# Dilated attention + S5 decoder layer: near values from a time-ordered copy of x, first weights in one transfer, last stores by halves

## The chip, the cores and the metric

One core of one Trainium2 chip runs the whole layer as a single program. The metric is device time in microseconds, the median of several executions. Engines are named as the profile names them: PE is TensorE (matmul; PEld its weight loads), DVE is VectorE, ACT is ScalarE, POOL is GpSimd, SP is SyncE, which here only issues DMAs.

## What is computed

A decoder layer on 512 tokens of width 1024. `x @ w_in` gives q, k and v for three dilation groups of attention (8 heads of 64 each), the input `u` of a state space model (SSM), and two sets of gate logits. Cut to what matters here:

```python
proj = x @ w_in[layer]
q, k, v = ...                      # (b, s, 3 groups, 8 heads, 64)
u, gate_logits = ...               # (b, s, 512), (b, s, 2, 1024)
for g, (window, dilation) in enumerate(((128, 1), (512, 4), (2048, 16))):
    o_g, lse_g = dilated_group_attention(q[:, :, g], k[:, :, g], v[:, :, g], window, dilation)
attn = sum over g of softmax(lse)_g * o_g
y_ssm = GLU(GELU(s5_ssm(u, ...))) @ w_ssm_br
h = layer_norm(ALPHA * x + (gates * (attn @ w_attn_br, y_ssm)) @ w_out)
x = layer_norm(ALPHA * h + (silu(h @ w_ff_gate) * (h @ w_ff_up)) @ w_ff_down)
```

Group 0 (window 128, dilation 1, "near") attends over tokens in the order of time, 128 at a time. Groups 1 and 2 attend over tokens of the same phase modulo 4 or 16.

## The kernel before, in words

**Tokens.** The host stores x with its tokens ordered by phase (time modulo 4). That is the order that groups 1 and 2 want. The near group wants time order, and the kernel reorders its q, k and v on the chip.

**Products.** Every product is done in a split form: a matrix is cut into a high half (rounded to fp32r) and a low half (the rest), and three matmuls `hi*hi`, `hi*lo`, `lo*hi` accumulate in one PSUM bank (`mm3`, lines 186 to 188). The function `split` makes the halves: ACT casts the high half (line 179), DVE subtracts it from the source to get the low half (line 180). For x and the first weights (of `u`) they are made at the start; for all other weights a class `Weights` loads units of 128x2048 by SP's queue into one of two `raw` buffers and splits each unit in two views `whi`/`wlo` of 128x1024, in three rotating slots. View n belongs to step n.

**Steps.** The table STEPS lists the projection tiles in the order of the program: steps 0 to 3 are `u` (done together by `u_tiles`), steps 4 to 7 the near values, steps 8 to 19 gates, then near k and q, then the other groups. Each step is 24 matmuls of 128x512 (`proj_tile`, or `v_tiles`). Other work is hung on steps by `at_step(n, ...)` and run by `run_fill(n)` in the middle of step n, or by `run_fill(n + 0.5)` at its end. Each engine executes its own instructions strictly in the order in which the program emits them.

**Near values before** (`v_near`, `v_turn`). Step 4 + hp makes 128 channels of v by 512 tokens in phase order (weights are the stationary operand, x the moving one). ACT copies the bank into time order (`vt`), and one step later PE transposes the four 128x128 blocks of `vt` into a bank `tv` (line 745), which ACT copies into `v`. The values of groups 1 and 2 are made by `v_tiles` instead: x blocks of 128 tokens are stationary, 512 columns of weights move, four banks are filled over four steps, and the result stands with tokens on the partitions, so nothing is transposed.

**The SSM's preparation** runs on DVE between these splits, as a list `late` of about two hundred small instructions (tiles `t16s`, `pw`, `bb`, then `zs`, `zd`, `ca`, `a`), of which `late.take` emits some now and then and `drip` a quota each half step. `make_pm` transposes `zs` on PE (16 transposes, tiles `pt`, line 522) and ACT copies them to `pmT`; `state_inputs` (tiles `sb`) needs `pmT` at the ends of steps 7 and 8.

**The end.** After the last matmul the last 128 rows are normalised: `norm_first` and `norm_second` are DVE instructions of 128x512, and `store` sends the rows in two halves of 64 by two queues. Before, the last quarter of the columns is scaled by ACT and finished by POOL (line 1265) while DVE does the rest.

Of the kernel before, what the change touches and what calls it, by code (L numbers as in the profile page):

```python
# [57 lines left out]
def as_phases(z):  # L58

    return z.rearrange("p (c r) -> p r c", r=4)  # L60
# [91 lines left out]
def emit(ctx, tc, i, out):  # L152
# [21 lines left out]
    dense, scores, turned, outs = ring(0, 1, 2), ring(3, 4), ring(5, 6), ring(7)  # L174
    pairs_ = ring(6, 7, 4, 5)

    def split(hi, lo, src, scale=None):
        if scale is None:
            act.copy(hi, src)  # L179
            dve.tensor_tensor(lo, src, hi.bitcast(F32), op=ALU.subtract)  # L180
        else:
            act.mul(hi, src, scale)  # L182
            dve.scalar_tensor_tensor(lo, src, scale, hi.bitcast(F32), op0=ALU.mult, op1=ALU.subtract)
# [40 lines left out]
    for n in range(2, N_GLU, 2):  # L224
        kind, g, un, _ = STEPS[n]
        if kind == "u":
            w.add(i["w_in"][1], 8)
        elif kind == "g":
            w.add(i["w_in"][20 + un], 8)
        else:  # L230
            w.add(i["w_in"][2 + 6 * g + 2 * "kqv".index(kind) + un], 2 if kind == "v" and g else 8)
    for un in range(2):
        w.add(i["w_glu"][un], 4)
    for un in range(4):
# [21 lines left out]
        queue.dma_start(wu[k0 // 4][:, k0 % 4 : k0 % 4 + k1 - k0],  # L256
                        i["w_in"][k0 // 4].rearrange("p (k c) -> p k c", k=4)[:, k0 % 4 : k0 % 4 + k1 - k0])

    for e in cols256:
        act.dma_start(wu[0][:, 0, e], i["w_in"][0][:, e])  # L260
    dve.memset(warm[:, 0:P], 0.0)
    act.activation(wact, warm[:, 0:1], AF.Exp)
    wb_ = dense("warm_b")
# [22 lines left out]
    zt = prep[:, 1024:2048]  # L286
    dmat = sa.tile([P, 8, 16], F32, name="dmat")
    sp.dma_start(sm, i["ssm_bc"])
    w.load()
    sp.dma_start(dmat, i["dmat"])  # L290
    sp.dma_start(bgate, i["bgate"])
    sp.dma_start(ident, i["ident"])
    sp.dma_start(rope, i["rope"])
    sp.dma_start(masks.rearrange("p n k -> p (n k)"), i["masks"].rearrange("p n k -> p (n k)"))

# [171 lines left out]
    for k in range(KT):  # L467
        if k == 0:

            (xh, uh), (xl, ul) = ((z[0][:, 0, :] for z in (xp[n], wup[n])) for n in range(2))  # L470
            xs, us = xr[0][:, 0:512], wu[0][:, 0, :]
            c0, c1 = cols256
            dve.tensor_copy(uh[:, c0], us[:, c0])
            act.copy(xh[:, c0], xs[:, c0])
            dve.tensor_copy(xh[:, c1], xs[:, c1])
            act.copy(uh[:, c1], us[:, c1])
            tt(xl, xs, xh.bitcast(F32), ALU.subtract)
            tt(ul, us, uh.bitcast(F32), ALU.subtract)
            late.take(4)
            continue  # L480
        split_x(k)
        split(wup[0][k // 4][:, k % 4], wup[1][k // 4][:, k % 4], wu[k // 4][:, k % 4])
        late.take(4 if k < 2 else 10)
# [248 lines left out]
        else:  # L732
            tt(dv[:, hp, :], cq, sw, ALU.add)

    def v_near(dv, ws, hp, mid):

        b = proj_tile(ws, f"pv0{hp}", mid)
        vt = at.tile([P, 512], F32, tag="cq", name=f"vt{hp}")
        act.copy(as_phases(vt), by_phase(b))
        return dv, vt, hp  # L740

    def v_turn(dv, vt, hp):
        b = turned(f"tv0{hp}")
        for blk in range(4):
            pe.transpose(b[:, 128 * blk : 128 * blk + 128], vt[:, 128 * blk : 128 * blk + 128], ident)
        act.copy(dv[:, :, 128 * hp : 128 * hp + 128], b.rearrange("p (b c) -> p b c", b=4))

    def v_tiles(dv, ws, j, g, mid):

        if j == 0:  # L750
            ssm["vb"] = [bank(7, f"pv{g}{tb}") if tb == 2 else dense(f"pv{g}{tb}") for tb in range(4)]
        for tb, b in enumerate(ssm["vb"]):
            if tb == 2:
                mid()
            for kk in range(2):
                k = 2 * j + kk
                mm3(b, kslice(xp, k, slice(128 * tb, 128 * tb + 128)), (ws[0][:, kk, :], ws[1][:, kk, :]), k == 0, k == KT - 1)
            if j == 3:
                act.copy(dv[:, tb, :], b)

# [175 lines left out]
    drip(9, 20, 1600)  # L936
    drip(20, 28, 500)
    at_step(3.5, u_turn)
    at_step(6, make_pm)
    for r in range(2):  # L940
        for m in range(2):
            at_step(7.5 + r, state_inputs, r, m)
# [39 lines left out]
    for hp in range(NPAIR):  # L982
        at_step((58, 59, 60, 61)[hp], merge_pair, hp)

    for _ in range(3):
        w.split()
        late.take(12)
    u_tiles()
    run_fill(3.5)
    for n in range(4, N_GLU):  # L990
        kind, g, un, c = STEPS[n]

        def mid(n=n):
            run_fill(n)

        if kind == "g":
            gate_tile(w.views[n], un, c, mid)
        else:
            if un == 0 and c == 0:
                dv = home({"k": (1, "g3", "g0"), "q": (8, 2, 1), "v": (3, "g1", 0)}[kind][g], f"{kind}{g}")  # L1000
                if qkv[g] is None:
                    qkv[g] = [None] * 3
                qkv[g]["qkv".index(kind)] = dv.rearrange("p (b c) -> p b c", b=4)
            dv = qkv[g]["qkv".index(kind)]
            if kind == "v" and g == 0:
                at_step(n + 1, v_turn, *v_near(dv, w.views[n], 2 * un + c, mid))
            elif kind == "v":
                v_tiles(dv, w.views[n], 2 * un + c, g, mid)
            else:
                qk_tile(dv, w.views[n], g, 2 * un + c, f"{kind}{g}", mid)  # L1010
        w.release()
        run_fill(n + 0.5)
# [244 lines left out]
    mv = mvs[NTT - 1]  # L1257
    dve.bn_aggr(mv[:, 0:2], bsts[NTT - 1])
    rstd(mv)
    for cs in reversed(halves):  # L1260
        norm_first(end, mv, lnb2, cs)

    cs = quarters[3]
    act.mul(end[:, cs], end[:, cs], mv[:, 3:4])
    pool.tensor_tensor(end[:, cs], end[:, cs], lnb2[:, 1, cs], op=ALU.add)
    for q, c in (((sp, act), halves[0]), ((act, sp), quarters[2])):
        norm_second(end, mv, lnb2, c)
        store(q, NTT - 1, end, c)
    store((sp, act), NTT - 1, end, cs)


def constants():
# [21 lines left out]
def layout(a):  # L1294
    x = a["x"][0][TOKENS]
    w = a["w_in"][0]
    hd = np.concatenate([np.arange(0, 16), np.arange(32, 48), np.arange(16, 32), np.arange(48, 64)])
    perm = (np.arange(NH)[:, None] * 64 + hd[None, :]).reshape(-1)
    parts = [w[:, 4608:5120]]
    for g in range(3):  # L1300
        parts.append(w[:, 1536 + 512 * g : 1536 + 512 * g + 512][:, perm])
        parts.append(w[:, 512 * g : 512 * g + 512][:, perm])
        parts.append(w[:, 3072 + 512 * g : 3072 + 512 * g + 512])
    parts.append(w[:, 5120:])

    def units(m, nk, cols):
        k, c = m.shape
        t = m.reshape(k // (nk * P), nk, P, c // cols, cols).transpose(0, 3, 2, 1, 4)
        return np.ascontiguousarray(t.reshape(-1, P, nk * cols))

    def pairs(m, nk, cols):
        k, c = m.shape
        t = m.reshape(nk, P, c // (2 * cols), 2, cols).transpose(2, 1, 3, 0, 4)
        return t.reshape(-1, P, 2 * nk * cols)

    glu = np.stack([a["w_glu"][0][:, :512].reshape(512, 4, P), a["w_glu"][0][:, 512:].reshape(512, 4, P)], 2)
    gu = np.stack([a["w_ff_gate"][0].reshape(D, NFF, P), a["w_ff_up"][0].reshape(D, NFF, P)], 2).reshape(D, 2 * DFF)
    parts = [units(p, 4, 512) if j in (0, 6, 9) else pairs(p, 8, P) for j, p in enumerate(parts)]

    def state(m):  # L1320
        return m.reshape(2, 8, 2, 64, *m.shape[2:]).transpose(2, 3, 1, 0, *range(4, m.ndim + 2)).reshape(P, NGP, *m.shape[2:])

    are, aim = state(a["ssm_a_re"][0]), state(a["ssm_a_im"][0])
    ldt = state(np.broadcast_to(a["ssm_log_dt"][0][:, None], (NG, 64)))
    br, bi = (state(a[n][0]).reshape(P, 256) for n in ("ssm_b_re", "ssm_b_im"))
    cr, ci = (state(a[n][0].transpose(0, 2, 1)).reshape(P, 256) for n in ("ssm_c_re", "ssm_c_im"))
    dm = np.zeros((4, 32, 8, 16), np.float32)
    d = a["ssm_d"][0].reshape(8, 4, 16)
    for h in range(16):
        dm[:, h, :, h] = d[:, :, h].T  # L1330
    xT = x.T.reshape(KT, P, S).transpose(1, 0, 2).reshape(P, KT * S)
    return {
        "x": x, "xT": xT, "w_in": np.concatenate(parts), "w_br": np.concatenate([units(a[n][0], 4, 256).reshape(2, 2, P, 1024).transpose(0, 2, 1, 3).reshape(2, P, 2048)
                                for n in ("w_ssm_br", "w_attn_br")]),
        "w_glu": pairs(glu.reshape(512, 1024), 4, 256), "w_out": units(a["w_out"][0], 4, 512)[[0, 2, 1, 3]],
        "w_gu": pairs(gu, 8, P), "w_dn": units(a["w_ff_down"][0], 2, 1024),
        "bgate": a["b_gate"][0].reshape(16, P).T, "ssm_small": np.stack([are, aim, ldt], 1),
        "ssm_bc": np.stack([np.stack([br, bi], 1), np.stack([cr, ci], 1)], 1),
        "dmat": dm.reshape(P, 8, 16), "ln1": np.stack([a["ln1_g"][0], a["ln1_b"][0]]),
        "ln2": np.stack([a["ln2_g"][0], a["ln2_b"][0]]),  # L1340
    }
# [24 lines left out]
```

## Time and profile before

| | us |
|---|---|
| median of 3 executions | 861.52 (861.26 to 861.63) |
| the profiled execution's own time | 861.88 |
| its span, first to last instruction | 860.1 |
| PE busy in the span | 850.1 (99%) |
| DVE busy | 485.7 (56%) |
| ACT busy | 292.2 (34%) |
| POOL busy | 26.5 (3%) |

The span is what the trace shows; 1.78 us of the profiled execution lie around it. Positions in the trace are microseconds from the span's start. Shares of busy time are averages over the whole span and say little of one stage.

### The profile page before, as it was taken

How to read it: one execution, taken by the hardware profiler on the slowest of the kernel's cores; microseconds unless marked ns; L12 is line 12 of the kernel's file. 1: busy time of each engine (PE TensorE's matmuls, PEld its weight loads, DVE VectorE, ACT ScalarE, POOL GpSimd, SP SyncE). 2: the span in 40 equal slices, each digit the busy share in tenths (PEclk: the TensorE clock that was granted, in tenths of full speed). 3: DMA queues.
4: the chain of work that ended last, by engine and by line, in shares of the span. 5: the costliest groups of instructions: out<-in, count | busy, mean ns of one | idle time of the engine just before them, and what ended most of it. 6: DMA issues, size and time to landing. Idle time of an engine off the chain costs nothing.

```text
span 860.1 us, 11317 instructions
## 1 busy us (share of the span) xinstructions
PE 850.1 (99%) x4586; PEld 701.6 (82%) x4586; DVE 485.7 (56%) x948; ACT 292.2 (34%) x477; POOL 26.5 (3%) x28
## 2 busy tenths in 40 slices
PE   9999999999999999999999999999999999999996
PEld 7878888887778888888888898888888888888885
DVE  7965899974665546356795863444433444222237
ACT  5364331155443344553251342222222222211111
POOL 0000000000000000000000600000000000000005
PEclk9999999999999999999999999999999999999999
DMA  9723421325121312112624142222222222322204
GB/s 340 189 83 105 122 98 50 125 89 180 50 98 51 101 62 86 50 56 92 244 99 147 50 147 98 98 98 98 94 93 94 92 92 94 136 96 96 95 0 98
DMA packets 24628, 90.06 MB, mean 105 GB/s; under 512 B 6400, under 2 KB 11264, under 8 KB 15488
## 3 DMA queue, kind: packets, MB, share of 16 engines
q1 hardware_dynamic: 22704, 86.59, 29.4%
q10 hardware_dynamic: 1872, 2.74, 0.9%
q8 instruction: 36, 0.59, 0.3%
q14 instruction: 16, 0.13, 0.0%
HBM read 84.87 MB, written 4.46 MB: 104 GB/s over the span
## 4 chain that ended last, share of the span: by engine, by line
PE 93%; DVE 3%; DMA 2%; ACT 1%; issue 0%; SPq 0%; DVEq 0%; ACTq 0%
PE fg L188 9%; PE fg L186 9%; PE fg L187 9%; PE dn L187 4%; PE dn L188 4%; PE dn L186 4%; PE pg L186 3%; PE pg L187 3%; PE pg L188 3%; PE pk L188 3%; PE pq L187 3%; PE pq L188 3%; PE pk L187 3%; PE pk L186 3%; PE pq L186 3%; PE pv L186 2%
## 5 line engine op out<-in xcount | busy, mean ns | idle before, releaser
L180 DVE TENSOR_TENSOR wlo<-raw,whi 128x1024 fp32r<-128x1024 f32 x134 | 164.3, 1227 | 200.1 <-ACT whi L179 200.0
L179 ACT CAST whi<-raw 128x1024 fp32r<-128x1024 f32 x134 | 140.1, 1047 | 221.5 <-PE dn L188 73.3
L186 PE MATMUL fg<-hh,whi 128*128 128x512 f32 (+1 forms) x376 | 141.3, 376 | 0.0
L187 PE MATMUL fg<-hl,whi 128*128 128x512 f32 (+1 forms) x376 | 141.2, 375 | 0.0
L188 PE MATMUL fg<-hh,wlo 128*128 128x512 f32 (+1 forms) x376 | 141.2, 375 | 0.0
L187 PEld LDWEIGHTS fg<-hl,whi 128*128 128x128 f32 x376 | 70.8, 188 | 12.9
L188 PEld LDWEIGHTS fg<-hh,wlo 128*128 128x128 f32 x376 | 70.8, 188 | 12.8
L186 PEld LDWEIGHTS fg<-hh,whi 128*128 128x128 f32 x376 | 70.8, 188 | 12.7
L187 PE MATMUL dn<-wlo,ff 128*128 128x512 f32 x168 | 65.4, 389 | 0.0
L186 PE MATMUL dn<-whi,ff 128*128 128x512 f32 x168 | 65.4, 389 | 0.0
L188 PE MATMUL dn<-whi,ff 128*128 128x512 f32 x168 | 65.4, 389 | 0.0
L186 PE MATMUL pg<-x_hi,whi 128*128 128x512 f32 x128 | 50.7, 396 | 0.0
L187 PE MATMUL pg<-x_lo,whi 128*128 128x512 f32 x128 | 49.9, 390 | 0.0
L188 PE MATMUL pg<-x_hi,wlo 128*128 128x512 f32 x128 | 49.9, 390 | 0.0
L182 ACT ACTIVATE ff<-fth 128x512 fp32r<-128x512 f32 x22 | 14.0, 634 | 102.7 <-DVE fth L315 102.7
L315 DVE TENSOR_TENSOR fth<-fth,fg 128x512 f32<-128x512 f32 x22 | 15.1, 687 | 56.9 <-PE fg L188 56.8
L791 ACT ACTIVATE pt<-pt,st 128x256 f32<-128x256 f32 (+1 forms) x64 | 31.0, 485 | 43.5 <-DVE st L789 43.5
L186 PE MATMUL pk<-x_hi,whi 128*128 128x512 f32 x96 | 37.8, 394 | 0.0
L186 PE MATMUL pq<-x_hi,whi 128*128 128x512 f32 x96 | 37.8, 394 | 0.0
L188 PE MATMUL pk<-x_hi,wlo 128*128 128x512 f32 x96 | 37.4, 390 | 0.0
L188 PE MATMUL pq<-x_hi,wlo 128*128 128x512 f32 x96 | 37.4, 390 | 0.0
L187 PE MATMUL pq<-x_lo,whi 128*128 128x512 f32 x96 | 37.4, 389 | 0.0
(261 smaller groups left out, 1464.6 us busy)
## 6 DMA issues: line engine op xcount, KB each, us to landing
raw<-in_w_in SPq DMA_DIRECT2D x26, 1024.0 KB, 4.8
raw<-in_w_gu SPq DMA_DIRECT2D x22, 1024.0 KB, 4.7
raw<-in_w_dn SPq DMA_DIRECT2D x11, 1024.0 KB, 4.8
raw<-in_w_br SPq DMA_DIRECT2D x4, 1024.0 KB, 4.7
raw<-in_w_out SPq DMA_DIRECT2D x4, 1024.0 KB, 4.7
raw<-in_w_glu SPq DMA_DIRECT2D x2, 1024.0 KB, 4.8
xn<-in_x SPq DMA_DIRECT2D x2, 1024.0 KB, 7.9
out_dram<-hn SPq DMA_DIRECT2D x13, 128.0 KB, 2.3
```

The source lines that it names most:

```text
L179: act.copy(hi, src)
L180: dve.tensor_tensor(lo, src, hi.bitcast(F32), op=ALU.subtract)
L182: act.mul(hi, src, scale)
L186: pe.matmul(dst, a[0], b[0], start=first, stop=False)
L187: pe.matmul(dst, a[0], b[1], start=False, stop=False)
L188: pe.matmul(dst, a[1], b[0], start=False, stop=last)
L315: eng.tensor_tensor(o, a, b, op=op)
L791: act.activation(pt[:, :n], pt[:, :n], AF.Exp, bias=mneg, scale=-1.0, accum_out=zsum)
```

## The change

Four edits. (1) The near values are made by `v_tiles`, like the others; their x blocks come from a second copy of x, `in_xT_time`, 2 MB in time order, loaded in two transfers into `xt_raw` and split into `xth`/`xtl`. For these the low halves are subtracted by POOL (`eng=pool`), four instructions of 128x1024. `v_near` and `v_turn` go, and with them 16 transposes and 8 copies on ACT (4 copies come in their place). (2) The third split of weights (view 6) moves from before `u_tiles` to the middle of step 4, the second half of the time-ordered x is split in the middle of steps 4 and 5, and `make_pm` moves from step 6 to 6.5. (3) The first weights of `u` come in one transfer instead of two, and DVE's first two casts change places. (4) The last rows are finished by DVE alone, in two halves, each stored when it is done.

```diff
@@ -174,10 +174,10 @@
     dense, scores, turned, outs = ring(0, 1, 2), ring(3, 4), ring(5, 6), ring(7)
     pairs_ = ring(6, 7, 4, 5)
 
-    def split(hi, lo, src, scale=None):
+    def split(hi, lo, src, scale=None, eng=dve):
         if scale is None:
             act.copy(hi, src)
-            dve.tensor_tensor(lo, src, hi.bitcast(F32), op=ALU.subtract)
+            eng.tensor_tensor(lo, src, hi.bitcast(F32), op=ALU.subtract)
         else:
             act.mul(hi, src, scale)
             dve.scalar_tensor_tensor(lo, src, scale, hi.bitcast(F32), op0=ALU.mult, op1=ALU.subtract)
@@ -228,7 +228,7 @@
         elif kind == "g":
             w.add(i["w_in"][20 + un], 8)
         else:
-            w.add(i["w_in"][2 + 6 * g + 2 * "kqv".index(kind) + un], 2 if kind == "v" and g else 8)
+            w.add(i["w_in"][2 + 6 * g + 2 * "kqv".index(kind) + un], 2 if kind == "v" else 8)
     for un in range(2):
         w.add(i["w_glu"][un], 4)
     for un in range(4):
@@ -256,8 +256,7 @@
         queue.dma_start(wu[k0 // 4][:, k0 % 4 : k0 % 4 + k1 - k0],
                         i["w_in"][k0 // 4].rearrange("p (k c) -> p k c", k=4)[:, k0 % 4 : k0 % 4 + k1 - k0])
 
-    for e in cols256:
-        act.dma_start(wu[0][:, 0, e], i["w_in"][0][:, e])
+    load_u(0, 1, act)
     dve.memset(warm[:, 0:P], 0.0)
     act.activation(wact, warm[:, 0:1], AF.Exp)
     wb_ = dense("warm_b")
@@ -286,10 +285,24 @@
     zt = prep[:, 1024:2048]
     dmat = sa.tile([P, 8, 16], F32, name="dmat")
     sp.dma_start(sm, i["ssm_bc"])
+
+
+    xt_raw = [home(h, f"xt_raw{j}") for j, h in enumerate((2, "g2"))]
+    xt = [], []
+
+    def split_time(j, u):
+        if u == 0:
+            for z, n, h in zip(xt, "hl", ((4, 6)[j], (5, 7)[j])):
+                z.append(big(h, f"xt{n}{j}", F32R).rearrange("p (k t) -> p k t", k=4))
+        hi, lo = (z[j][:, 2 * u : 2 * u + 2, :].rearrange("p k t -> p (k t)") for z in xt)
+        split(hi, lo, xt_raw[j][:, 1024 * u : 1024 * u + 1024], eng=pool)
+
+    sp.dma_start(xt_raw[0], i["xT_time"][0])
     w.load()
     sp.dma_start(dmat, i["dmat"])
     sp.dma_start(bgate, i["bgate"])
     sp.dma_start(ident, i["ident"])
+    sp.dma_start(xt_raw[1], i["xT_time"][1])
     sp.dma_start(rope, i["rope"])
     sp.dma_start(masks.rearrange("p n k -> p (n k)"), i["masks"].rearrange("p n k -> p (n k)"))
 
@@ -470,9 +483,9 @@
             (xh, uh), (xl, ul) = ((z[0][:, 0, :] for z in (xp[n], wup[n])) for n in range(2))
             xs, us = xr[0][:, 0:512], wu[0][:, 0, :]
             c0, c1 = cols256
-            dve.tensor_copy(uh[:, c0], us[:, c0])
             act.copy(xh[:, c0], xs[:, c0])
             dve.tensor_copy(xh[:, c1], xs[:, c1])
+            dve.tensor_copy(uh[:, c0], us[:, c0])
             act.copy(uh[:, c1], us[:, c1])
             tt(xl, xs, xh.bitcast(F32), ALU.subtract)
             tt(ul, us, uh.bitcast(F32), ALU.subtract)
@@ -732,19 +745,6 @@
         else:
             tt(dv[:, hp, :], cq, sw, ALU.add)
 
-    def v_near(dv, ws, hp, mid):
-
-        b = proj_tile(ws, f"pv0{hp}", mid)
-        vt = at.tile([P, 512], F32, tag="cq", name=f"vt{hp}")
-        act.copy(as_phases(vt), by_phase(b))
-        return dv, vt, hp
-
-    def v_turn(dv, vt, hp):
-        b = turned(f"tv0{hp}")
-        for blk in range(4):
-            pe.transpose(b[:, 128 * blk : 128 * blk + 128], vt[:, 128 * blk : 128 * blk + 128], ident)
-        act.copy(dv[:, :, 128 * hp : 128 * hp + 128], b.rearrange("p (b c) -> p b c", b=4))
-
     def v_tiles(dv, ws, j, g, mid):
 
         if j == 0:
@@ -754,7 +754,7 @@
                 mid()
             for kk in range(2):
                 k = 2 * j + kk
-                mm3(b, kslice(xp, k, slice(128 * tb, 128 * tb + 128)), (ws[0][:, kk, :], ws[1][:, kk, :]), k == 0, k == KT - 1)
+                mm3(b, kslice(xp if g else xt, k, slice(128 * tb, 128 * tb + 128)), (ws[0][:, kk, :], ws[1][:, kk, :]), k == 0, k == KT - 1)
             if j == 3:
                 act.copy(dv[:, tb, :], b)
 
@@ -936,7 +936,7 @@
     drip(9, 20, 1600)
     drip(20, 28, 500)
     at_step(3.5, u_turn)
-    at_step(6, make_pm)
+    at_step(6.5, make_pm)
     for r in range(2):
         for m in range(2):
             at_step(7.5 + r, state_inputs, r, m)
@@ -982,11 +982,16 @@
     for hp in range(NPAIR):
         at_step((58, 59, 60, 61)[hp], merge_pair, hp)
 
-    for _ in range(3):
+    for u in range(2):
         w.split()
         late.take(12)
+        split_time(0, u)
+    late.take(12)
     u_tiles()
     run_fill(3.5)
+    at_step(4, w.split)
+    for u in range(2):
+        at_step(4 + u, split_time, 1, u)
     for n in range(4, N_GLU):
         kind, g, un, c = STEPS[n]
 
@@ -1002,9 +1007,7 @@
                     qkv[g] = [None] * 3
                 qkv[g]["qkv".index(kind)] = dv.rearrange("p (b c) -> p b c", b=4)
             dv = qkv[g]["qkv".index(kind)]
-            if kind == "v" and g == 0:
-                at_step(n + 1, v_turn, *v_near(dv, w.views[n], 2 * un + c, mid))
-            elif kind == "v":
+            if kind == "v":
                 v_tiles(dv, w.views[n], 2 * un + c, g, mid)
             else:
                 qk_tile(dv, w.views[n], g, 2 * un + c, f"{kind}{g}", mid)
@@ -1257,16 +1260,11 @@
     mv = mvs[NTT - 1]
     dve.bn_aggr(mv[:, 0:2], bsts[NTT - 1])
     rstd(mv)
-    for cs in reversed(halves):
+    for cs in halves:
         norm_first(end, mv, lnb2, cs)
-
-    cs = quarters[3]
-    act.mul(end[:, cs], end[:, cs], mv[:, 3:4])
-    pool.tensor_tensor(end[:, cs], end[:, cs], lnb2[:, 1, cs], op=ALU.add)
-    for q, c in (((sp, act), halves[0]), ((act, sp), quarters[2])):
-        norm_second(end, mv, lnb2, c)
-        store(q, NTT - 1, end, c)
-    store((sp, act), NTT - 1, end, cs)
+    for q, cs in zip(((sp, act), (act, sp)), halves):
+        norm_second(end, mv, lnb2, cs)
+        store(q, NTT - 1, end, cs)
 
 
 def constants():
@@ -1315,7 +1313,7 @@
 
     glu = np.stack([a["w_glu"][0][:, :512].reshape(512, 4, P), a["w_glu"][0][:, 512:].reshape(512, 4, P)], 2)
     gu = np.stack([a["w_ff_gate"][0].reshape(D, NFF, P), a["w_ff_up"][0].reshape(D, NFF, P)], 2).reshape(D, 2 * DFF)
-    parts = [units(p, 4, 512) if j in (0, 6, 9) else pairs(p, 8, P) for j, p in enumerate(parts)]
+    parts = [units(p, 4, 512) if j in (0, 3, 6, 9) else pairs(p, 8, P) for j, p in enumerate(parts)]
 
     def state(m):
         return m.reshape(2, 8, 2, 64, *m.shape[2:]).transpose(2, 3, 1, 0, *range(4, m.ndim + 2)).reshape(P, NGP, *m.shape[2:])
@@ -1329,8 +1327,9 @@
     for h in range(16):
         dm[:, h, :, h] = d[:, :, h].T
     xT = x.T.reshape(KT, P, S).transpose(1, 0, 2).reshape(P, KT * S)
+    xT_time = units(a["x"][0].T, 4, S)
     return {
-        "x": x, "xT": xT, "w_in": np.concatenate(parts), "w_br": np.concatenate([units(a[n][0], 4, 256).reshape(2, 2, P, 1024).transpose(0, 2, 1, 3).reshape(2, P, 2048)
+        "x": x, "xT": xT, "xT_time": xT_time, "w_in": np.concatenate(parts), "w_br": np.concatenate([units(a[n][0], 4, 256).reshape(2, 2, P, 1024).transpose(0, 2, 1, 3).reshape(2, P, 2048)
                                 for n in ("w_ssm_br", "w_attn_br")]),
         "w_glu": pairs(glu.reshape(512, 1024), 4, 256), "w_out": units(a["w_out"][0], 4, 512)[[0, 2, 1, 3]],
         "w_gu": pairs(gu, 8, P), "w_dn": units(a["w_ff_down"][0], 2, 1024),
```

DVE, around the third and fourth low halves of weights (`wlo2_6` belongs to step 6, `wlo0_7` to step 7; `t16s`, `pw`, `bb`, `zs`, `zd` are the SSM's preparation). Before, where `wlo2_6` stands, and then where `wlo0_7` stands:

```order
L180 TENSOR_TENSOR wlo1_5_278<-raw2_122,whi1_5_277 128x1024
L76 SCALAR_TENSOR_TENSOR t16s_137<-t16s_137 128x16
L76 TENSOR_TENSOR t16s_137<-t16s_137 128x16 x2
L76 TENSOR_SCALAR t16s_137<-t16s_137 128x16 x2
L76 TENSOR_TENSOR t16s_137<-t16s_137 128x16 x7
L180 TENSOR_TENSOR wlo2_6_296<-raw3_130,whi2_6_295 128x1024
L76 TENSOR_TENSOR t16s_137<-t16s_137 128x16 x2
```

```order
L76 TENSOR_TENSOR zs_247<-bb_142,pw_83 128x8x64
L76 TENSOR_TENSOR zd0_245<-bb_142,pw_83 128x512
L76 TENSOR_TENSOR zs_247<-zs_247,zd0_245 128x8x64
L76 TENSOR_TENSOR zs_247<-bb_142,pw_83 128x8x64
L180 TENSOR_TENSOR wlo0_7_479<-raw3_130,whi0_7_478 128x1024
L76 TENSOR_TENSOR zd0_245<-bb_142,pw_83 128x512
```

Of the change, at the second place:

```order
L76 TENSOR_TENSOR zs_250<-bb_145,pw_83 128x8x64
L76 TENSOR_TENSOR zd0_248<-bb_145,pw_83 128x512
L76 TENSOR_TENSOR zs_250<-zs_250,zd0_248 128x8x64
L76 TENSOR_TENSOR zs_250<-bb_145,pw_83 128x8x64
L180 TENSOR_TENSOR wlo2_6_473<-raw3_132,whi2_6_472 128x1024
L180 TENSOR_TENSOR wlo0_7_493<-raw3_132,whi0_7_492 128x1024
L76 TENSOR_TENSOR zd0_248<-bb_145,pw_83 128x512
```

The low half for step 6 has moved behind the rest of the SSM's preparation up to the fourth `zs` instruction, directly ahead of the one for step 7; nothing else on DVE moved in between.

POOL, from its first work to the first norm of the layer, before and then of the change:

```order
L527 MEMSET zer_250 16x48
L836 MEMSET wt_2635 128x4x96
L1078 MEMSET epsb_3955 128x1
L1082 ISA
L1082 TENSOR_TENSOR mva0_4103<-mva0_4103,epsb_3955 128x1
```

```order
L540 MEMSET zer_253 16x48
L180 ISA
L180 TENSOR_TENSOR xtl0_281<-xt_raw0_129,xth0_280 128x1024 x2
L180 TENSOR_TENSOR xtl1_477<-xt_raw1_130,xth1_476 128x1024 x2
L836 MEMSET wt_2622 128x4x96
L1081 MEMSET epsb_3942 128x1
```

POOL, which had nothing between its first memset and `wt`, now has four subtractions of two SBUF operands there.

PE, around the transposes of `zs` (`pt`), before and then of the change:

```order
L188 MATMUL pv02_538<-x_hi0_91,wlo2_6_296 128x512
L522 MATMUL pt0_561<-ident_86,zs_247 128x128 x4
L522 MATMUL pt1_567<-ident_86,zs_247 128x128 x4
L522 MATMUL pt2_573<-ident_86,zs_247 128x128 x4
L522 MATMUL pt3_579<-ident_86,zs_247 128x128 x4
L745 MATMUL tv01_585<-ident_86,vt1_523 128x128 x4
L186 MATMUL pv02_538<-x_hi1_92,whi2_6_295 128x512
```

```order
L188 MATMUL pv03_455<-whi2_6_472,xtl1_477 128x512
L535 MATMUL pt0_592<-ident_86,zs_250 128x128 x4
L535 MATMUL pt1_598<-ident_86,zs_250 128x128 x4
L535 MATMUL pt2_604<-ident_86,zs_250 128x128 x4
L535 MATMUL pt3_610<-ident_86,zs_250 128x128 x4
L186 MATMUL pv00_452<-whi0_7_492,xth1_476 128x512
```

The transposes of `zs` stood in the middle of step 6, followed by those of `tv`; they now stand between steps 6 and 7, and those of `tv` are gone.

## Rows read from the trace of the kernel before

**Rows 1.** The page: span, then each engine's busy time, share and instruction count.

```profile
span 860.1 us, 11317 instructions
PE 850.1 (99%) x4586; PEld 701.6 (82%) x4586; DVE 485.7 (56%) x948; ACT 292.2 (34%) x477; POOL 26.5 (3%) x28
```

**Rows 2.** Timeline of PE, steps 4 to 8: start, duration, engine, line, operation, tiles, shape.

```profile
27.56 0.39 PE L186 MATMUL pv<-x_hi,whi 128*128 128x512 f32 x1
...
35.49 0.39 PE L188 MATMUL pv<-x_hi,wlo 128*128 128x512 f32 x1
35.72 0.60 PE L745 MATMUL tv<-ident,vt 128*128 128x128 f32 x4
...
36.39 0.40 PE L187 MATMUL pv<-x_lo,whi 128*128 128x512 f32 x1
...
41.42 0.39 PE L188 MATMUL pv<-x_hi,wlo 128*128 128x512 f32 x1
...
45.02 0.39 PE L187 MATMUL pv<-x_lo,whi 128*128 128x512 f32 x1
...
53.26 0.39 PE L188 MATMUL pv<-x_hi,wlo 128*128 128x512 f32 x1
...
58.15 0.39 PE L188 MATMUL pg<-x_hi,wlo 128*128 128x512 f32 x1
...
59.37 0.39 PE L187 MATMUL pg<-x_lo,whi 128*128 128x512 f32 x1
```

**Rows 3.** Waits from 27 to 62 us: who waited for whom, total, times, longest.

```profile
PEld tv L745 <- ACT sst L603: 0.5, 1, 0.5
PEld pt L522 <- DVE zs L76: 0.5, 1, 0.5
```

**Rows 4.** Windows: stretch, length, busy time of each engine (instructions), PE clock, DMA.

```profile
23.00:35.60 12.60, 12.60 (x57) 10.43 (x56) 12.53 (x64) 4.00 (x6) 0.00 (x0) 1.00 0.52 186
35.60:42.00 6.40, 6.32 (x31) 4.93 (x29) 6.30 (x11) 2.54 (x3) 0.00 (x0) 1.00 1.28 155
```

**Rows 5.** Timeline of DVE: the fourth low half of weights, the last `zs`.

```profile
35.63 1.22 DVE L180 TENSOR_TENSOR wlo<-raw,whi 128x1024 fp32r<-128x1024 f32 x1
...
41.35 0.69 DVE L76 TENSOR_TENSOR zs<-zs,zd 128x512 f32<-128x512 f32 x1
```

**Rows 6.** Timeline of DVE and POOL in the first layer norm.

```profile
476.63 1.49 DVE L180 TENSOR_TENSOR wlo<-raw,whi 128x1024 fp32r<-128x1024 f32 x1 [1.22 <-ACT whi L179]
477.12 2.15 POOL L1109 TENSOR_TENSOR hn<-hn,lnb 128x512 f32<-128x512 f32 x1
...
489.29 0.75 DVE L312 SCALAR_TENSOR_TENSOR hn<-hn,mva,lnb 128x512 f32<-128x512 f32 x1
...
491.69 1.29 POOL L1109 TENSOR_TENSOR hn<-hn,lnb 128x512 f32<-128x512 f32 x1
491.71 1.81 DVE L312 SCALAR_TENSOR_TENSOR hn<-hn,mva,lnb 128x512 f32<-128x512 f32 x1
```

**Rows 7.** Timeline of the end: last rows on DVE and POOL, last store.

```profile
854.63 0.75 DVE L312 SCALAR_TENSOR_TENSOR hn<-hn,mvb,lnb 128x512 f32<-128x512 f32 x1
854.88 1.07 POOL L1265 TENSOR_TENSOR hn<-hn,lnb 128x256 f32<-128x256 f32 x1 [0.62 <-ACT hn L1264]
855.30 0.94 DVE L312 SCALAR_TENSOR_TENSOR hn<-hn,mvb,lnb 128x256 f32<-128x256 f32 x1
...
856.89 0.75 ACTq L1214 DMA_DIRECT2D out_dram<-hn  x1
```

**Rows 8.** Timeline of the start: waits for first weights, SSM inputs, second weight unit.

```profile
6.11 0.30 PEld L577 LDWEIGHTS pu<-x_hi,wuh 128*128 128x128 f32 x2 [0.65 <-ACT wuh L476]
...
7.60 0.17 DVE L76 TENSOR_SCALAR t16s<-small 128x16 f32<-128x16 f32 x1 [0.82 <-DMA small<-in_ssm_small]
...
21.51 1.05 ACT L179 CAST whi<-raw 128x1024 fp32r<-128x1024 f32 x1 [1.83 <-DMA raw<-in_w_in]
```

**Rows 9.** Windows after the last matmul; PE clock is the column before the last two.

```profile
851.00:852.00 1.00, 0.79 (x7) 0.59 (x5) 0.81 (x3) 0.00 (x0) 0.92 (x2) 1.00 0.65 154
855.00:856.00 1.00, 0.00 (x0) 0.00 (x0) 1.00 (x2) 0.00 (x0) 0.96 (x1) 0.96 0.36 82
```

## The prediction

> **What bounds the kernel now.** I read the page first, then the timeline of PE over steps 4 to 8, the waits and the busy time by stretch of the same steps, and last the two ends of the trace. The page says that PE is busy 99% of the span [rows 1], so a change pays only if it takes time out of PE's own stream or off the two ends. In the stage of the near values that stream is plain: 35 matmuls lie between the starts at 27.56 and 35.49, which is 0.2266 us each [rows 2], and steps 4 to 7 are 96 of them. What interrupts them can be read off as well, from the start of the last matmul ahead of an interruption to that of the second one behind it, less two pitches of 0.2266. The first transposes of `tv` cost 36.39 - 35.49 - 0.45 = 0.45 us. Those of `zs` with the second `tv` cost 45.02 - 41.42 - 0.45 = 3.15. The fourth `tv`, in step 8, costs 59.37 - 58.15 - 0.45 = 0.77 with its wait for ACT [rows 2, 3]. The last matmul of v starts at 53.26, so the stage ends at 53.49.
>
> The reader should see a second engine there. DVE is busy 12.53 of 12.60 us from 23.0 to 35.6, and 6.30 of 6.40 up to 42.0 [rows 4], with instructions that nearly all read two tiles in SBUF. PE already waits 0.5 us for DVE's `zs` [rows 3]. So DVE has no slack up to the last `zs`, which ends at 41.35 + 0.69 = 42.04 [rows 5]. Its 56% of the span hides this.
>
> **Edit 1, PE's side.** Steps 4 to 7 stay 96 matmuls of 128x512, which I take at the same 0.2266. The 16 transposes of `tv` go: 4 x 0.45 = 1.8 us, and the waits around them. By the same price the 16 transposes of `zs`, which stay, need 1.79 of their 3.15. ACT gains too (four copies for eight), but it isn't the bound. With PE alone in view, steps 4 to 6 would run from 27.3 (see edit 3) for 72 x 0.2266 = 16.3 us to 43.6, the `zs` transposes to 45.4, step 7 to 50.85, against 53.49: 2.64 us gained, and 0.77 more in step 8.
>
> **Edit 1, data.** The time-ordered x takes the place of the second weight unit in SP's queue. That unit's split began at 21.51 [rows 8], so the first `xth` should too, and POOL can begin at about 22.6, 5 us ahead of step 4. The next unit lands some 3 us later and is now split in step 4, so the 2 MB more are hidden. I cost them at nothing. If they came 4 us later PE would wait about 1.5 us at step 4, time that it loses anyway two steps on.
>
> **Edit 1, POOL.** Four subtractions of 128x1024, both operands in SBUF, run beside the gapless stream of DVE. The trace of before has this pairing on a small scale. At 491.71 a DVE instruction with two SBUF operands took 1.81 us, while a twin of it took 0.75; POOL had begun one of 1.29 us at 491.69 [rows 6]. DVE stood still for 1.06 of these 1.29. At 477.12 it was POOL's turn to wait: 2.15 instead of 1.29, until DVE's low half that began at 476.63 was done [rows 6]. At the end of the kernel POOL's instruction of 256 columns came at 854.88 into a running DVE instruction, took 1.07, and DVE's next one, issued at 855.30 right behind, took 0.94 although half as many columns as 0.75 should take some 0.4 [rows 7]. So POOL waits for the instruction that runs and then goes ahead of the next: a gapless DVE doesn't keep it out. A POOL instruction of 512 columns holds DVE for 1.06 to 1.29 us, by these rows; one of 1024 I take as twice that, 2.1 to 2.6, and choose 2.3. Four of them are 9.2 us on DVE.
>
> The Trainium skill, page "SBUF — State Buffer", section "Who interferes with whom", has this as a rule: DVE with two SBUF inputs and a GpSimd instruction that reads SBUF share a port pair under an exclusive lock, and the one that starts first keeps it for the whole instruction. Taken to the letter the hold is the whole 2.6 us, and the sum below becomes about 1.2 us longer. The trace agrees in kind (1.06 of 1.29).
>
> **Edit 2.** Before, the low half of view 6 was done long before its step. Now it stands directly ahead of that of view 7. An instruction that is moved past others leaves the end of the group where it was, so the low half of view 6 ends where that of view 7 began, at 35.63, and the last `zs` still ends at 42.04 [rows 5]. PE wants view 6's low half with the second matmul of step 6, at 27.3 + 49 x 0.2266 = 38.4, and `zs` at 43.6. So the slack is 2.8 and 1.6 us, enough with DVE undisturbed, and far too little for 9.2. All four POOL instructions come early enough to count: the first two from 22.6 on, the other two after ACT's casts in steps 4 and 5, at about 31 and 34, ahead of a low half that is late by then.
>
> **The sum.** DVE may start 0.3 us earlier, since its inputs `small`, for which it waited 0.82 [rows 8], are issued sooner on ACT. View 6's low half then ends at 35.63 - 0.3 + 9.2 = 44.5, and PE stands still from 38.4, 6.1 us. Step 6 ends at 49.8. `zs` ends at 42.04 - 0.3 + 9.2 = 50.9, another 1.1 us of waiting. Then 1.79 for the transposes and 5.44 for step 7: 58.2 against 53.49, 4.7 us later. Step 8 gives back 0.77. DVE is late by more than PE from then on, but its next low half is needed only at step 8, and it had pauses there.
>
> **PE's clock.** After the last matmul, which ended at about 851.8, the granted clock stayed full until the window from 855 to 856, whose mean is 0.96: it fell to 1.2 GHz some 4.1 us after PE went quiet [rows 9]. A wait of 6.1 us is longer than that. If all of the rest of step 6 ran at the lower level, it would take 5.2 us more, of which the wait for `zs` covers 1.1: so 0 to 4.1 us. No row shows how long the lower level lasts under load; I take 0.5, near the lower end.
>
> **Edit 3.** PE waited 0.65 us for the second half of the first weights [rows 8]. One transfer may end that, or may land as late as the second half did and then lose the two matmuls that ran ahead of it: a gain of 0.65 to a loss of 0.45. I take 0.25. It decides nothing, since the wait in step 6 swallows it.
>
> **Edit 4.** DVE's second half follows at 855.38 and takes 0.75 with no POOL beside it, so the last store is issued at about 856.1 instead of 856.89 [rows 7], twice as large. I take 0.55 us off (bounds 0.2 and 0.8).
>
> Together: +4.7 - 0.77 - 0.55 + 0.5 = +3.9 us on the profiled execution (span 860.1, time 861.88). The median of the runs is 0.36 below that time; I add the 3.9 to the median: 865.4. Holds of 2.1 and no loss by the clock give 864.1; holds of 2.6 and 2 us by the clock give 868.1. That is the likeliest case's own range.
>
> **Rivals.** *POOL's work is hidden* (the other side): DVE isn't held, or only between its instructions. Then PE bounds, and the sum is -2.64 - 0.77 - 0.55 = -4.0, so 857.5. It needs all four holds together under 1.9 us; the change loses from 5.9 us on, 1.5 per instruction. For it speaks that many DVE instructions here are tiny; against it, all three pairings in rows 6 and 7. *Holds of 1.1 to 1.8 us each*, if a large POOL instruction lets DVE in halfway: 859.9 to 863.2, no change to speak of. *POOL is kept out* until DVE first pauses, behind view 6's low half at about 35.6, where it waits for step 4. Then step 4's third matmul waits for POOL's first low half until about 38.2 instead of 27.8: v ends near 61.3, and the time is 868 to 870. Against it speaks 854.88 in rows 7.
>
> **Chances.** Likeliest case 0.62, POOL kept out 0.08, halfway 0.13, hidden 0.17. Slower by over 0.2% (1.7 us, about what a measurement of this kernel tells from no change) 0.70, within it 0.13, faster 0.17. The range leaves out the hidden case and the far end of POOL kept out: 859.9 to 869.0.
>
> **What would show it.** In the profile after: a pause of PE of about 6 us at the second matmul of step 6, ended by DVE's `wlo`; DVE instructions of 2 us and more where 0.17 to 1.2 is usual, each beside a POOL row of the time-ordered x; the transposes of `zs` waiting for DVE; a lower granted clock after the pause. I am wrong if DVE's rows keep their lengths from 22 to 38 us, if PE runs through steps 4 to 7 without a pause, or if POOL's rows are far shorter than 2.3 us.

## Result and the profile after

The changed kernel takes 865.61 us (median of 6 executions, 864.83 to 866.93) against 861.68 of the kernel before beside it (6 executions, 861.26 to 861.89): a ratio of 1.0047, 95% interval 1.0034 to 1.0060. It is slower, by 3.9 us. The profiled execution took 865.04.

The page of the changed kernel gives span, busy time and share:

```profile
span 863.3 us, 11285 instructions
PE 849.7 (98%) x4570; PEld 701.5 (81%) x4570; DVE 494.1 (57%) x948; ACT 292.0 (34%) x476; POOL 36.1 (4%) x31
```

Beside [rows 1], PE has 16 instructions fewer and yet a span 3.2 us longer, POOL is busy 9.6 us more, and DVE 8.4 us more with the same 948 instructions. That last pair is what to follow up: DVE's count of instructions did not grow, so some of them got longer. The timeline of POOL from 15 to 70 us (start, duration, engine, line, operation, tiles, shape) shows the four new subtractions:

```profile
22.41 5.33 POOL L180 TENSOR_TENSOR xtl<-xt_raw,xth 128x1024 fp32r<-128x1024 f32 x2 [21.55 <-DMA raw<-in_w_in]
32.18 2.47 POOL L180 TENSOR_TENSOR xtl<-xt_raw,xth 128x1024 fp32r<-128x1024 f32 x1 [4.43 <-ACT xth L179]
35.74 2.81 POOL L180 TENSOR_TENSOR xtl<-xt_raw,xth 128x1024 fp32r<-128x1024 f32 x1 [1.10 <-ACT xth L179]
```

The timeline of DVE of the changed kernel, in the same columns, at the four places beside them and at the two instructions that PE needs:

```profile
21.85 1.22 DVE L180 TENSOR_TENSOR wlo<-raw,whi 128x1024 fp32r<-128x1024 f32 x1
22.98 2.40 DVE L76 SCALAR_TENSOR_TENSOR t16s<-t16s 128x16 f32<-128x16 f32 x1
25.39 2.39 DVE L76 SCALAR_TENSOR_TENSOR t16s<-t16s 128x16 f32<-128x16 f32 x1
...
32.17 0.18 DVE L76 TENSOR_TENSOR pw<-pw,ptmp 128x16 f32<-128x16 f32 x1
32.27 2.40 DVE L76 TENSOR_TENSOR t16s<-t16s 128x16 f32<-128x16 f32 x1
34.60 0.18 DVE L76 TENSOR_TENSOR pw<-pw,ptmp 128x16 f32<-128x16 f32 x1
...
35.85 0.41 DVE L76 TENSOR_TENSOR bb<-t16s,prep 128x256 f32<-128x256 f32 x1
36.18 2.42 DVE L76 TENSOR_TENSOR ptmp<-pw 128x32 f32<-128x32 f32 x1
...
42.36 2.35 DVE L180 TENSOR_TENSOR wlo<-raw,whi 128x1024 fp32r<-128x1024 f32 x2
...
49.20 0.69 DVE L76 TENSOR_TENSOR zs<-zs,zd 128x512 f32<-128x512 f32 x1
```

Instructions of 16 or 32 columns, 0.16 to 0.18 us each on either side, take 2.39 to 2.42 beside each POOL instruction: four holds of 2.24, 8.95 us together. So the low half of view 6, which is the first of the two that begin at 42.36, ends at 43.58 and the last `zs` at 49.89. The waits from 20 to 66 us (who waited for whom, total, times, longest) hold one on PE that [rows 3] does not have:

```profile
PEld pv L187 <- DVE wlo L180: 4.8, 1, 4.8
PE pv L187 <- DVE wlo L180: 4.3, 1, 4.3
```

The timeline of PE shows where it stands, and what the engine does after it:

```profile
28.02 0.39 PE L186 MATMUL pv<-whi,xth 128*128 128x512 f32 x1
...
38.90 0.39 PE L186 MATMUL pv<-whi,xth 128*128 128x512 f32 x1
43.63 0.50 PE L187 MATMUL pv<-wlo,xth 128*128 128x512 f32 x1 [4.34 <-DVE wlo L180]
...
44.43 0.63 PE L187 MATMUL pv<-wlo,xth 128*128 128x512 f32 x1
44.86 0.63 PE L188 MATMUL pv<-whi,xtl 128*128 128x512 f32 x1
...
47.84 0.40 PE L186 MATMUL pv<-whi,xth 128*128 128x512 f32 x1
...
50.60 1.91 PE L535 MATMUL pt<-ident,zs 128*128 128x128 f32 x16
52.26 0.48 PE L186 MATMUL pv<-whi,xth 128*128 128x512 f32 x1
...
57.57 0.39 PE L188 MATMUL pv<-whi,xtl 128*128 128x512 f32 x1
```

Step 6's second matmul starts 4.73 us behind its first, which is a pause of 4.5. From 44.43 to 47.84 eight matmuls follow at 0.427 us each instead of 0.2266 [rows 2]: 1.6 us lost. The windows of the same stretch (length, busy time and instructions of each engine, then PE's clock, DMA share and GB/s) give the reason:

```profile
38.00:44.40 6.40, 2.06 (x9) 1.42 (x8) 6.37 (x13) 1.04 (x1) 0.55 (x1) 1.00 0.92 124
44.40:47.90 3.50, 3.50 (x10) 2.69 (x9) 3.43 (x7) 0.00 (x0) 0.00 (x0) 0.51 1.17 184
```

The granted clock is 0.51 there, the lower of its two levels (1.2 GHz). The last matmul of v starts at 57.57; with one pitch of 0.23 v ends at 57.57 + 0.23 = 57.80 instead of 53.49, so 4.31 later. At the kernel's end the last matmul starts at 855.03, and DVE finishes alone:

```profile
855.03 0.28 PE L188 MATMUL dq<-whi,ff 128*128 128x256 f32 x1
...
856.63 2.73 DVE L325 SCALAR_TENSOR_TENSOR hn<-hn,mvb,lnb 128x512 f32<-128x512 f32 x4
```

From that matmul's start to the end of the span it is now 863.3 - 855.03 = 8.27 us, against 860.1 - 851.51 = 8.59 in the trace of before [rows 1], whose timeline of PE ends with this matmul:

```profile
851.51 0.28 PE L188 MATMUL dq<-whi,ff 128*128 128x256 f32 x1
```

### The profile page after: what moved, and what is told of

Same layout as the page of the kernel before. It is cut to its first block, busy times and chain, and to the rows that moved or that the text cites. A ratio compares the mean times of both kernels' runs of the same rounds, so it can differ in the third digit from the quotient of the medians.

```text
span 863.3 us, 11285 instructions
## 1 busy us (share of the span) xinstructions
PE 849.7 (98%) x4570; PEld 701.5 (81%) x4570; DVE 494.1 (57%) x948; ACT 292.0 (34%) x476; POOL 36.1 (4%) x31
## 4 chain that ended last, share of the span: by engine, by line
PE 94%; DVE 4%; DMA 1%; issue 0%; ACT 0%; SPq 0%; DVEq 0%
PE fg L186 9%; PE fg L187 9%; PE fg L188 9%; PE dn L188 4%; PE dn L186 4%; PE dn L187 4%; PE pg L186 3%; PE pg L187 3%; PE pg L188 3%; PE pk L186 3%; PE pk L188 3%; PE pq L188 3%; PE pq L186 3%; PE pq L187 3%; PE pk L187 3%; PE pv L186 2%
```

## Experiments

The theory (*port*): POOL's four subtractions keep DVE from SBUF for 9 us while it has no slack, and PE pays for it at the first DVE result that it needs. The rivals: the place of view 6's low half in the program (*place*), the 2 MB more to load (*traffic*), and the edits at start and end. Each kernel was timed beside the kernel before on the same chip, the first four on one (861.48 us) and the last four on another (861.52).

**x1: DVE subtracts.** All else as in the changed kernel.

```diff
-        split(hi, lo, xt_raw[j][...], eng=pool)
+        split(hi, lo, xt_raw[j][...], eng=dve)
```

> The changed kernel with the four subtractions of the time-ordered x on DVE instead of POOL, nothing else. Theory (POOL holds DVE through each of its four instructions, about 2.24 us each, 8.95 in all): DVE now has 4 x 1.14 = 4.56 us of work of its own in place of the holds, only two of them ahead of the low half of view 6, which then ends near 36.9, before PE wants it at 38.9. The pause in step 6 and the lower clock behind it are gone, PE waits about 1.2 us for zs instead, and the time is 860.0 to 860.8. Rival (the place of view 6's low half behind the SSM's preparation is the cause, POOL costs nothing): DVE has 4.56 us more to do and the pause grows or stays, 865.5 to 870.

Measured: 858.94 us (858.74 to 860.53), ratio 0.9973 [0.9963, 0.9983]. DVE has more real work than in the changed kernel, four instructions of 1.22 us on a saturated engine, and the kernel is 6.7 us faster. In the waits and the timeline of DVE of this kernel:

```profile
PE pt L535 <- DVE zs L76: 0.3, 1, 0.3
```

```profile
35.81 1.22 DVE L180 TENSOR_TENSOR wlo<-raw,whi 128x1024 fp32r<-128x1024 f32 x1
36.95 1.22 DVE L180 TENSOR_TENSOR xtl<-xt_raw,xth 128x1024 fp32r<-128x1024 f32 x1
...
43.80 0.69 DVE L76 TENSOR_TENSOR zs<-zs,zd 128x512 f32<-128x512 f32 x1
44.41 1.22 DVE L180 TENSOR_TENSOR xtl<-xt_raw,xth 128x1024 fp32r<-128x1024 f32 x1
```

View 6's low half ends at 37.03, ahead of its step, though its place in the program is that of the changed kernel: *place* alone is not the cause. It came out 1 us better than expected since the fourth subtraction stands behind the last `zs` in DVE's order (44.41): only three of the four delay `zs`, which ends at 44.49 instead of 49.89 - 8.95 + 4.56 = 45.50 and is late by 0.3 us only. So the gain has two parts that x1 does not separate: a subtraction costs DVE 1.13 us instead of 2.24, and by the program's order two of the four stand behind view 6's low half, while POOL's four all ran ahead of it.

**x2: ACT makes the low half**, by copying `x_lo`, which is already there, into time order (8 copies of 128x512); two buffers change places for it.

```diff
...
-        split(hi, lo, xt_raw[j][...], eng=pool)
+        for k in range(2):
+            act.copy(as_phases(lo[:, k, :]), by_phase(xp[1][j][:, 2 * u + k, :].bitcast(F32)))
+        act.copy(hi.rearrange("p k t -> p (k t)"), xt_raw[j][...])
```

> The low half of the time-ordered x is not subtracted at all: ACT copies it, reordered, from the low half of x that exists already (eight copies of 128x512 with a step of four in the output). POOL has nothing in this stage and DVE nothing new. Theory (port): DVE's rows keep their lengths, view 6's low half ends near 34.6, PE runs steps 4 to 7 without a pause, 858.4 to 859.2; the loss of 0.46 us at the start stays. Rival (place of view 6's low half): a pause in step 6 of 2 us or more stays, 861 to 865. If ACT with its eight copies of about 1 us is late, the pause is ended by ACT and lies at the start of step 4 or 5.

Measured: 858.25 us (858.18 to 858.95), ratio 0.9964 [0.9951, 0.9976], the fastest kernel here, 3.2 us under the kernel before. ACT had the room: its copies take 1.11 to 1.15 us each and PE waits for nothing from 20 to 60 us. By form of instruction (duration min, median, max, first and last start), and on PE's timeline:

```profile
L299 ACT CAST xtl<-x_lo x8: 1111/1128/1146, 19.4 to 35.2; 128x512 fp32r<-128x512 f32 x8
```

```profile
43.81 1.91 PE L537 MATMUL pt<-ident,zs 128*128 128x128 f32 x16
```

**x3: no second split.** This kernel leaves out the splitting of the time-ordered x, on ACT and POOL, and takes the blocks of `xp` in its place (so near values come out in the wrong order of tokens); the 2 MB are still loaded.

```diff
-                mm3(b, kslice(xp if g else xt, k, ...
+                mm3(b, kslice(xp, k, ...
...
-        split_time(0, u)
+        pass
...
-    for u in range(2):
-        at_step(4 + u, split_time, 1, u)
```

> Leaves out the split of the time-ordered x: the stationary blocks are those of the phase-ordered x, so the near values stand in the wrong order of tokens; the 2 MB are still loaded. This is the floor of edit 1 with its traffic. Theory (port): 858.4 to 859.0, no pause on PE up to step 8. Rival (the 2 MB more of transfers delay something): the time stays above 860 and PE or ACT waits for a DMA between 20 and 45 us.

Measured: 858.47 us (858.07 to 860.32), ratio 0.9968 [0.9957, 0.9979], and no wait on PE in the stage. *Traffic* is not the cause: the 2 MB are still loaded, and with POOL's work gone so is the pause. What the load itself costs is not measured, as no run leaves it out. x2, which does all the work, is as fast: on ACT the low half is hidden whole.

**x4: view 6's low half early again**, POOL as in the changed kernel.

```diff
         split_time(0, u)
+    w.split()
     late.take(12)
     u_tiles()
-    at_step(4, w.split)
```

> The third split of weights (view 6) goes back ahead of the u tiles, POOL keeps its four subtractions. Theory (port): the pause leaves step 6 but zs still ends near 50, since DVE loses the same 8.95 us ahead of it; PE arrives at its transposes near 44.3 and waits there some 5 us, with a lower clock behind it: 864.0 to 866.0. Rival (place of view 6's low half): the pause is gone, 858.5 to 860.5.

Measured: 866.36 us (866.1 to 867.72), ratio 1.0061 [1.0048, 1.0073]. Its waits, its timeline of PE and a window (columns as above):

```profile
PE pt L535 <- DVE zs L76: 5.2, 2, 3.8
```

```profile
48.04 0.47 PE L535 MATMUL pt<-ident,zs 128*128 128x128 f32 x1 [3.77 <-DVE zs L76]
49.98 3.46 PE L535 MATMUL pt<-ident,zs 128*128 128x128 f32 x15 [1.46 <-DVE zs L76]
```

```profile
47.30:54.10 6.80, 4.60 (x19) 4.12 (x20) 6.73 (x18) 2.34 (x4) 0.00 (x0) 0.50 0.24 99
```

The pause moves to the next DVE result that PE needs, `zs`, as *port* says; the clock then stays at its lower level for 6.8 us instead of 3.4. It came out 0.4 us above what was expected, for which the clock is the likely reason: the 15 transposes take 3.46 us here, against 1.86 in y3's trace at the full level (below).

**y3: the pause filled.** The changed kernel, with 18 matmuls of 128x512 whose result nothing reads, directly ahead of step 6.

```diff
+        if j == 2 and g == 0:
+            filler = bank(3, "filler")
+            for _ in range(18):
+                pe.matmul(filler, xp[0][0][:, 0, 0:128], xp[0][0][:, 0, :], start=True, stop=True)
```

> The changed kernel with 18 matmuls of 128x512 more (4.1 us of PE's work into a bank that nothing reads) directly ahead of step 6, so that PE works through most of its pause of 4.5 us. Everything that step 6 waits for stays as it was. Theory A, the pause itself is given by DVE's lateness (4.5 us) and the fall of the granted clock behind it adds 1.6 us in half of the runs and 3.0 to 3.2 in the other half: without the fall, 863.3 to 863.6 with a spread under 0.6, no row of step 6 at the pitch of .43 us, and step 6's second matmul still at 43 to 44 us. Theory B, the granted clock falls for another reason than the pause, or costs nothing: 864.8 to 867 as in the changed kernel.

Measured: 864.61 us (864.44 to 864.74), ratio 1.0036 [1.0024, 1.0049]. Four microseconds of matmuls were added and the kernel is 1.0 us faster in the median, 0.4 against the profiled execution. Its timeline of PE and the window behind the pause:

```profile
38.55 4.24 PE L755 MATMUL filler<-x_hi 128*128 128x512 f32 x18
42.63 0.39 PE L186 MATMUL pv<-whi,xth 128*128 128x512 f32 x1
43.84 0.50 PE L187 MATMUL pv<-wlo,xth 128*128 128x512 f32 x1 [0.83 <-DVE wlo L180]
...
49.20 0.27 PE L535 MATMUL pt<-ident,zs 128*128 128x128 f32 x1
50.17 1.86 PE L535 MATMUL pt<-ident,zs 128*128 128x128 f32 x15 [0.70 <-DVE zs L76]
```

```profile
44.40:47.90 3.50, 3.50 (x17) 2.88 (x16) 3.43 (x6) 0.00 (x0) 0.00 (x0) 1.00 0.98 215
```

The clock stays at its full level, so the pause is what made it fall. But the expected 863.3 to 863.6 was too low by 1 us: I had taken off all of the 1.6 us, and behind the faster step 6 PE now waits 0.7 us for `zs`, which the slow matmuls had covered in the changed kernel. From step 6's second matmul to the end of v it is 14.17 us in the changed kernel (43.63 to 57.80) and 13.50 in y3 (43.84 to 57.34), so the net price of the clock there is 0.67; on the whole 0.42 are left between the two profiled executions, since DVE's low half ended 0.21 later in y3. More may lie in the spread: three executions of the changed kernel lie from 864.83 to 865.04 with a mean granted clock of 0.996, three from 866.18 to 866.93 with 0.994, and all five of y3 within 0.3 us with 0.997 or 0.998. That isn't proof, for the executions of x1 spread over 1.8 us (858.74 to 860.53) and those of x3 over 2.3 (858.07 to 860.32), with a mean granted clock of 0.997 in the longest ones. No trace of one of the later three was taken; x4's trace shows what a longer low stretch looks like.

**y1 and y2: start and end alone**, in the kernel before.

```diff
-    for e in cols256:
-        act.dma_start(wu[0][:, 0, e], i["w_in"][0][:, e])
+    load_u(0, 1, act)
...
-            dve.tensor_copy(uh[:, c0], us[:, c0])
             act.copy(xh[:, c0], xs[:, c0])
             dve.tensor_copy(xh[:, c1], xs[:, c1])
+            dve.tensor_copy(uh[:, c0], us[:, c0])
```

> The kernel before with edit 3 alone (the first weights in one transfer, and the casts beside it in their new order). In the profile of after the first proper matmul started at 5.47 us (4.99 before) and step 4 at 28.02 (27.56 before). Theory A, the start of the changed kernel costs .46 us: 861.9 to 862.1 against 861.5 for before. Theory B, the prediction's term, a gain of .25: 861.2. Theory C, the start of a kernel varies by that much from execution to execution and the edit is worth nothing: 861.4 to 861.6, and step 4 at 27.5 to 27.8.

Measured: 861.49 us (861.12 to 862.04, 11 executions), ratio 1.0000 [0.9991, 1.0009].

```diff
-    for cs in reversed(halves):
+    for cs in halves:
         norm_first(end, mv, lnb2, cs)
...                                      # the last quarter's work on ACT and POOL goes
+    for q, cs in zip(((sp, act), (act, sp)), halves):
+        norm_second(end, mv, lnb2, cs)
+        store(q, NTT - 1, end, cs)
```

> The kernel before with edit 4 alone (the last tile normalized and stored by halves, all on DVE). In the profile of after the stretch behind the last matmul's start took 8.27 us instead of 8.59, so .3 less: 861.1 to 861.3 against 861.5. The prediction's term of .55 would give 860.9 to 861.0. If the end's edit hid a loss elsewhere: 861.5 or more.

Measured: 861.48 us (861.12 to 862.17, 11 executions), ratio 0.9999 [0.9991, 1.0008]. Neither edit is worth anything that 11 executions can tell from zero; the intervals allow 0.7 to 0.8 us either way, so that the predicted 0.25 and 0.55 are neither shown nor excluded. The first matmul of `u` starts at 5.17 in y1's trace (4.99 before, 5.47 in the changed kernel); step 4 starts at 27.48 in y1 and at 27.50 in y2. The median of y1 lies in the range of theory C of its expectation; its interval does not exclude A or B.

**y4: x2 with the start of the kernel before.**

```diff
-    load_u(0, 1, act)
+    for e in cols256:
+        act.dma_start(wu[0][:, 0, e], i["w_in"][0][:, e])
...                                      # the casts in their old order; ACT's copies as in x2
```

> x2_low_on_act (the low half of the time-ordered copy by ACT, 858.25 us) with the start of the kernel before: the first weights in two transfers and the casts in their old order. If the one transfer costs .46: 857.8 and below x2. If it gains .25: 858.5. If the start only varies from one execution to the next: 858.1 to 858.4. In each case below both kernels, by 3 us or more below the kernel before.

Measured: 858.79 us (858.57 to 859.1), ratio 0.9969 [0.9958, 0.9980]; no gain over x2, rather a loss of 0.5, though on another chip, and above all three ranges of the expectation. In its trace both halves of the weights came later than in the kernel before (their first casts start at 5.16 and 6.25 us, against 4.35 and 5.65), and PE stood twice:

```profile
5.80 0.70 PE L593 MATMUL pu<-x_hi,wuh 128*128 128x512 f32 x2 [0.96 <-DVE x_hi L491]
6.71 0.74 PE L593 MATMUL pu<-x_hi,wuh 128*128 128x512 f32 x2 [0.20 <-ACT wuh L492]
```

Step 4 began at 28.19 there and at 27.48 in x2. Whether one transfer is better once the rest of the change is in, or the start merely varied, one trace of each can't say; y1 shows no gain.

## Why the prediction was right, point by point

865.4 was predicted and 865.61 measured, by the mechanism that was forecast. The time of each profiled execution less the end of v in its trace shows where the time was lost and won:

| kernel | profiled, us | v ends | rest |
|---|---|---|---|
| before | 861.88 | 53.49 | 808.39 |
| y1, start alone | 861.47 | 53.02 | 808.45 |
| y2, end alone | 861.27 | 53.08 | 808.19 |
| changed | 865.04 | 57.80 | 807.24 |
| y3, pause filled | 864.62 | 57.34 | 807.28 |
| x4, early low half | 866.36 | 59.11 | 807.25 |
| x1, DVE | 859.02 | 51.70 | 807.32 |
| x3, no split | 858.47 | 51.17 | 807.30 |
| x2, ACT | 858.22 | 51.01 | 807.21 |
| y4, ACT, two transfers | 858.96 | 51.72 | 807.24 |

The rest is the same to 0.11 us wherever edit 1 is in. All differences between these seven are made before v ends.

- *PE's side of edit 1.* Without a hindrance (x2, x3) v ends 2.3 to 2.5 us earlier than in the trace of before; 2.64 was predicted, of which 0.25 were for the start. Against y1 and y2, which leave steps 4 to 7 as they were, it is 1.9 to 2.1: the profiled execution of before was a long one, 0.36 above the median that the prediction started from. The rest is 1.15 shorter, where step 8's `tv` (0.77) and the end (0.55) made 1.32. The pitch of 0.2266 and the prices of the transposes held.
- *POOL.* A hold of 2.24 us per instruction against the 2.3 taken, 8.95 in all against 9.2, by extrapolation from 1.06 of 1.29 us at half the size [rows 6]. In the trace DVE is held until POOL is done: POOL's row from 32.18 ends at 34.65, DVE's from 32.27 at 34.67. By the rule of the Trainium skill, page "SBUF — State Buffer", section "Who interferes with whom", the lock is held for the whole instruction; these rows agree. The 1.06 of 1.29 did not mean that DVE got in halfway: either time DVE lost about 0.23 us less than POOL's row lasts (2.24 of 2.47 here). As [rows 7] had shown, a gapless DVE does not keep POOL out, though it is not always the very next instruction that is held: behind POOL's start at 35.74, `bb` (35.85) still ran at its usual 0.41, and the one at 36.18 was held. x1, x2 and x3 take POOL away in three ways, and the pause goes each time.
- *The pause* was predicted at 6.1 us and is 4.5. Three terms of its sum were mis-sized, all in the same direction: DVE's start (0.3 earlier predicted; 1.1 measured, `wlo` at 21.85 against 22.97), the holds (0.25 less), and PE's arrival at step 6's second matmul (39.13 instead of 38.4, since step 4 started at 28.02 and not at 27.3).
- *The wait for `zs`* (1.1 predicted) doesn't show in the changed kernel, since the clock made step 6 so slow that `zs` was there first; y3, with the clock kept up, has it with 0.7.
- *The clock* was taken at 0.5 (0 to 4.1), less what the wait for `zs` would cover. It slowed eight matmuls by 1.6 us in all, and its net price, by y3, is 0.67 up to the end of v and 0.42 in the profiled execution. The 1.0 between the medians is not shown to be the clock's alone.
- *Edit 2* moved the pause, as said, and did not make it: with the low half early (x4) the same delay ends in the next wait.
- *Edits 3 and 4*, -0.25 and -0.55, are the terms for which no run speaks: y1 and y2 show no difference and allow either term. In the traces the end is 0.2 to 0.3 us shorter.
- *The sum* on the profiled execution was 861.88 + 3.9 = 865.78, against 865.04: v's end was put 0.9 us too late (4.7 and 0.5, against 4.31), and the rest 0.17 too short. The median stands 0.57 above this execution, by the three longer ones; that the forecast meets it to 0.2 us is in part chance.

Of the rivals, *hidden* (857.5) comes near what x2 measures with ACT in POOL's place (858.25, which is 3.2 us below the kernel before and not 4.0). *Halfway* and *kept out* have the rows against them: holds of 2.24 us, the first of them at 22.98.

## What to carry to other kernels

Before work is handed to an idle POOL, look at what DVE does beside it: where DVE runs without gaps, a POOL instruction on SBUF is added to DVE's own time at POOL's slower price (2.24 us here, against 1.13 from start to start if DVE does it itself, x1), and as soon as POOL's inputs are there, not where the program's order would put it on DVE. ACT made the same tile by copies, and PE waited for none of them (x2). And when a busy engine loses time, list the results that others want from it in order: undoing the first wait only moves the loss to the next one, and a pause of PE can be paid for twice, by its length and by the clock behind it.

## What was not expected of the hardware

- A DVE instruction of 16 columns took 2.40 us because POOL had started beside it; in a list by line this hides in a mean. Not only instructions that combine two tiles are held: in x4's trace it was a TENSOR_SCALAR of 16 columns (25.60, 2.37 us).
- After the pause of 4.5 us the granted clock stayed full for the first three matmuls and fell only then, for 3.4 us (eight matmuls of 0.427 us); in x4 it fell during the wait, some 3 us after the last matmul (windows 47.00:47.30 and 47.30:48.00 at 0.96 and 0.50), for 6.8 us. The executions of the changed kernel differ by up to 2.1 us and those of y3 by 0.3; those of x3 differ by 2.3 with the clock up, so the spread is not shown to come from the clock.
- The first matmul of `u` starts at 4.99 to 5.18 us in the three traces without edit 1 (before, y1, y2) and at 5.47 to 5.80 in the seven with it, with the first weights in one transfer or in two (y4). Step 4 starts at 27.48 to 27.56 without it and at 27.48 to 28.19 with it, not always together: in y3 5.80 and 27.67, in the changed kernel 5.47 and 28.02. Whether the 2 MB more are the reason no run shows.
